# A two-layer hybrid trunk: a larger landing constant in the order planner, and another buffer for layer 2's SGU constants

## The chip, the cores and the metric

The kernel runs on one core of one Trainium2 chip. The metric is the device time of one execution in microseconds, the median of several runs. Four engines compute: TensorE (PE, whose weight loads the profile lists apart as PEld), VectorE (DVE), ScalarE (ACT) and GpSimd (POOL). SyncE (SP) issues all transfers of the program, and each engine works through its own queue in the order in which the program was written.

## The reference

Two layers act on 512 latent positions (x) and 256 context positions (ctx), with 1024 channels. The second layer still reads the context but does not produce it anew. Each layer computes, cut to what matters:

```python
h = x * (1 + scale) + shift                  # scale, shift, gate from silu(c) @ w_ada
parts = split(h @ w_in)                      # q,k,v, GLA, SGU and merge-gate columns
y_attn = attention(q, concat(k_ctx, k), concat(v_ctx, v)) * silu(a_g)
y_gla  = rms_norm(gla_forward + gla_backward) * silu(g_g)
vn     = layer_norm(s_v, sgu_ln_g, sgu_ln_b)
y_sgu  = s_u * (einsum('gts,bnsgc->bntgc', sgu_w, vn) + sgu_b) * silu(s_g)
m = sigmoid(m_a)*(y_attn@w_br_attn) + sigmoid(m_g)*(y_gla@w_br_gla) + sigmoid(m_s)*(y_sgu@w_br_sgu)
x_new = layer_norm(alpha * x + gate * (m @ w_out), post_g, post_b)
```

All of it is float32 in and out.

## The kernel before

**Matmuls.** Each float32 operand is split into a high part and a low rest in the matmul's faster float32 form, and each product is made of three matmuls (hi·hi, hi·lo, lo·hi; `mm3`). A weight slab is 256 rows by 256 columns (256 KB). `wgroup` loads it into one of three `raw` buffers, ACT writes `hi`, DVE writes `lo`, and after that the raw buffer takes the next slab; `hi` and `lo` have five buffers each.

**Order of the work.** Nothing is issued as it is written. The class `Sched` records every instruction with its reads, writes and a reckoned duration (`_cost`), and `Sched.order` simulates the five engines: at each step the engine that is free first takes the ready instruction with the smallest priority. 16 rounds are run (`issue`); after each the priorities move towards the latest start times of that round, and the round with the shortest reckoned end is issued. The order on every engine's queue is thereby fixed; on the chip an instruction at the head of a queue waits for its semaphores, and everything behind it on that engine waits too. A transfer is reckoned like this (L325 to L328; `cost` is bytes / 335 ns):

```python
            if e == "SP":
                dma = max(dma, st + 1300.0) + cost
                free[e] = max(st + 60.0, dma - self.AHEAD)
                end = dma + 700.0
```

`end` is when the readers of the loaded tile may start, and when a buffer whose last use is a store comes free. What else reads `end` is the backward pass that makes the latest start times.

**Places.** SBUF tiles live in places named by tags (`T(tag, ...)`), each with a fixed number of buffers (`BUFS`, L515: `hc` 2, `raw` 3, `S3` 8, most others 1). Tiles take the buffers of a tag strictly in the order in which the code first uses them; a tile whose tag is full waits until an earlier one has had its last use. What bears on the change:

- `T3` (one buffer), layer 2: `yat` (L909, the attention's output, until it is split into `yh` and `yl` for its projection), then `sgc` (L1226), then `mac0` (L1254, the first half of the merge's sum), then `pg` (L1375).
- `hc` (two buffers): the high and low half of the context's modulated rows (`new_h`, L707; layer 2's are `hch` and `hcl`, read by layer 2's projections for keys, values and GLA), and after them, in layer 2, `pgx` (L1313, the post-norm constants of layer 1).
- `T1`: `gv` (GLA's values) and then `ymix` (the SGU's result). `T5`: `kT`, then `sv` (the SGU's input read back from DRAM), then the merge's second half.
- `S3` (eight buffers): among much else, in this order, the kept gate rows read back from DRAM: 4 of `agd`, 4 of `ggd`, 4 of `sud`, 4 of `sgd` (all named `kept`), and then, for the first branch of the merge, rows of w_ada (`wada`) and `kept` from `md` (the gate rows of the merge's first branch).

**The SGU and the merge of a layer.** `sgc` holds four rows of constants, `lg`, `lb`, `bs` and `wsT`, each a transfer of 256 KB. For each of four 128-position tiles DVE makes statistics of `sv`, subtracts and scales, multiplies by `lg` and adds `lb` (both `sv<-sv,sgc`); PE multiplies by `wsT` (`pt<-sgc,sv`); DVE adds `bs` into `ymix`. Then `ymix` is multiplied by `kept` of `sud` and of `sgd`. The merge's first branch multiplies the projection of `yat` by the sigmoid of `kept` from `md` into `mac0`. Rows of w_ada are multiplied on DVE beside the merge (`ada_dot`: `prod` and `wada`).

The page's line numbers are those of helpers for most instructions (L421 records a call, L128 one of two engines' choice, L119 a group of matmuls), so the views are read by tile names.

Of the kernel before, what the change touches and what calls it, by code (L numbers as in the profile page):

```python
# [22 lines left out]
C_GQ, C_GK, C_GV, C_GG = 1280, 1536, 1792, 2336  # L23
C_SU, C_SV, C_SG = 2848, 3360, 3872
C_MA, C_MG, C_MS = 4384, 5408, 6432


class Sched:
# [109 lines left out]
    def order(self, prio):  # L138
# [31 lines left out]
        dma, cur, ticks, acted = 0.0, None, {}, 0.0  # L170
# [45 lines left out]
        while done < n:  # L216
# [108 lines left out]
            if e == "SP":  # L325
                dma = max(dma, st + 1300.0) + cost
                free[e] = max(st + 60.0, dma - self.AHEAD)
                end = dma + 700.0  # L328
            else:
                end = free[e] = st + cost  # L330
                if e == "ACT":
                    acted = end
                if e in held and e in self.port[i]:
                    held[e] = end
# [170 lines left out]
def kernel(ctx: ExitStack, tc: tile.TileContext, A, out, dbg=None):  # L505
# [11 lines left out]
    def T(tag, shape, dt=F32, name=None):  # L517
        return sc.tile(sb, shape, dt, tag, BUFS.get(tag, 1), name or tag, "SB")
# [192 lines left out]
    def layer(l, X, start=None):  # L711
        full = l == 0
# [510 lines left out]

        lab(f"{l}sgu")

        sgc = T("T3", [128, 4, 512], name="sgc")  # L1226
        lg, lb, bs, wsT = (sgc[:, i] for i in range(4))
        SP.dma_start(out=lg, in_=A["sgu_ln_g"][l].partition_broadcast(128))
        SP.dma_start(out=lb, in_=A["sgu_ln_b"][l].partition_broadcast(128))
# [227 lines left out]
    def start0():  # L1457
# [100 lines left out]
        return st_b  # L1558

    X1 = layer(0, X0, start0)  # L1560
    layer(1, X1)
    with tc.manual_schedule():
        a = 0
# [73 lines left out]
```

## Time and profile before

| | |
|---|---|
| median of 3 runs | 1430.35 us (1429.0 to 1435.49) |
| the profiled execution's own time | 1431.16 us |
| its span, first to last instruction | 1429.3 us |
| mean granted TensorE clock | 0.996 |
| instructions | 27382 |
| moved by transfers | 168.55 MB, mean 118 GB/s |

The layers follow one another: layer 1's start, attention and GLA until about 450 us, its merge and output until about 850, then layer 2's attention until about 1025, its GLA until about 1165, its SGU and merge until about 1380 and its output to the end. An engine's idle time in brackets, with an arrow and a name, is how long the engine stood still before that instruction and what ended it. Matmuls are pipelined, their ends are modelled; a PE that counts as busy may still run at the lower of its two clock levels, which a row of a window shows as PEclk.

### The profile page before, as it was taken

What the parts mean: (1) busy time and instruction counts of PE and PEld (TensorE: products, weight loads), DVE (VectorE), ACT (ScalarE), POOL (GpSimd) and SP (SyncE); (2) the same over time, 40 slices, a digit from 0 to 9 for tenths busy, and PEclk for the clock granted to TensorE, in tenths of its full rate; (3) what the DMA queues carried; (4) which work ended last, traced back from release to release, by engine and by line L of the source; (5) the groups of instructions that cost most, each with busy time, mean ns of one, the idle gap of its engine ahead of it and who ended that gap; (6) DMA issues with size and microseconds to landing.
All of it is one profiled execution on the core that took longest, in us unless ns stands there. A gap on an engine that the chain in (4) does not pass through costs nothing.

```text
span 1429.3 us, 27382 instructions
## 1 busy us (share of the span) xinstructions
PE 1387.9 (97%) x10724; PEld 1227.5 (86%) x10724; DVE 1032.5 (72%) x2206; ACT 671.3 (47%) x1293; POOL 164.5 (12%) x261
## 2 busy tenths in 40 slices
PE   8999999999999999999999999999999998999997
PEld 5798899987888888888889999998987877888887
DVE  8968877897977678732147684897799876645396
ACT  4566667844464323212232174666774554422331
POOL 0021100034330000000000020110014320000003
PEclk9999999999999999999999999999999999999999
DMA  9410012332356765521224232112243467535542
GB/s 321 160 45 9 23 31 65 124 94 64 93 177 207 250 200 169 158 67 45 65 77 148 66 119 71 30 31 60 82 148 90 117 193 252 168 97 177 182 144 94
DMA packets 123956, 168.55 MB, mean 118 GB/s; under 512 B 9497, under 2 KB 90801, under 8 KB 123825
## 3 DMA queue, kind: packets, MB, share of 16 engines
q1 hardware_dynamic: 123826, 166.79, 37.4%
q8 instruction: 84, 1.38, 0.4%
q14 instruction: 46, 0.38, 0.1%
HBM read 143.41 MB, written 23.34 MB: 117 GB/s over the span
## 4 chain that ended last, share of the span: by engine, by line
PE 73%; DVE 16%; DMA 5%; issue 2%; ACT 2%; POOL 1%; SPq 0%; POOLq 0%; DVEq 0%; ACTq 0%
PE p L421 60%; PE pt L421 8%; PE s L421 4%; DVE M L128 3%; DVE lo L128 2%; DMA wada<-in_w_adaT_dram 2%; DVE wada L421 1%; DVE sm L421 1%; DVE junk L421 1%; DMA raw<-in_w_in_dram 1%; PE s L119 1%; DVE PTs L421 1%; DMA sgc<-in_sgu_b_dram 1%; DVE cs L421 1%; POOL sf L421 0%
## 5 line engine op out<-in xcount | busy, mean ns | idle before, releaser
L128 DVE TENSOR_TENSOR lo<-raw,hi 128x512 fp32r<-128x512 f32 (+1 forms) x293 | 202.4, 700 | 173.7 <-ACT hi L421 166.2
L421 ACT ACTIVATE hi<-raw 128x512 fp32r<-128x512 f32 (+1 forms) x296 | 185.8, 634 | 233.2 <-PE p L421 149.8
L421 PE MATMUL p<-hlh,hi 128*128 128x512 f32 x704 | 280.9, 399 | 2.5 <-DVE mac L421 1.5
L421 PE MATMUL p<-hlh,lo 128*128 128x512 f32 x704 | 280.7, 399 | 1.5 <-DVE lo L128 1.3
L421 PE MATMUL p<-hll,hi 128*128 128x512 f32 x704 | 278.6, 396 | 0.0
L421 PEld LDWEIGHTS p<-hlh,lo 128*128 128x128 f32 x704 | 132.4, 188 | 31.6 <-DVE lo L128 2.1
L421 PEld LDWEIGHTS p<-hlh,hi 128*128 128x128 f32 x704 | 132.3, 188 | 29.8 <-ACT hi L421 2.2
L421 PEld LDWEIGHTS p<-hll,hi 128*128 128x128 f32 x704 | 132.3, 188 | 26.5
L421 PE MATMUL p<-hch,lo 128*128 128x256 f32 x368 | 104.5, 284 | 0.0
L421 PE MATMUL p<-hch,hi 128*128 128x256 f32 x368 | 104.2, 283 | 0.0
L421 PE MATMUL p<-hcl,hi 128*128 128x256 f32 x368 | 104.0, 283 | 0.0
L421 PE MATMUL p<-hi,hlh 128*128 128x256 f32 (+1 forms) x352 | 102.0, 290 | 0.0
L421 PE MATMUL p<-hi,hll 128*128 128x256 f32 (+1 forms) x352 | 100.8, 286 | 0.0
L421 PE MATMUL p<-lo,hlh 128*128 128x256 f32 (+1 forms) x352 | 99.8, 284 | 0.0
L421 POOL TENSOR_SCALAR sf<-sf 128x1 f32<-128x1 f32 x20 | 7.5, 374 | 642.3 <-DVE sf L421 641.9
L421 PE MATMUL p<-yh,hi 128*128 128x512 f32 (+1 forms) x192 | 70.0, 364 | 7.8 <-DVE mac L421 6.7
L421 ACT ACTIVATE P<-s,sm 128x768 f32<-128x768 f32 (+1 forms) x80 | 65.4, 821 | 23.5 <-DVE sm L421 23.2
L421 DVE TENSOR_REDUCE sm<-s 128x1 f32<-128x768 f32 (+1 forms) x72 | 65.0, 921 | 12.4 <-PE s L421 12.2
L421 DVE TENSOR_TENSOR PTs<-pt,PTs 128x512 fp32r<-128x512 f32 x104 | 69.2, 685 | 4.1 <-ACT PTs L421 3.1
L421 PEld LDWEIGHTS p<-hcl,hi 128*128 128x128 f32 x368 | 69.3, 188 | 2.1
L421 PEld LDWEIGHTS p<-hch,hi 128*128 128x128 f32 x368 | 69.5, 189 | 1.9
L421 DVE SCALAR_TENSOR_TENSOR wada<-wada,srow 128x512 f32<-128x512 f32 x96 | 65.1, 687 | 8.0 <-DMA wada<-in_w_adaT_dram 6.7
(299 smaller groups left out, 3352.1 us busy)
## 6 DMA issues: line engine op xcount, KB each, us to landing
raw<-in_w_in_dram SPq DMA_DIRECT2D x204, 256.0 KB, 3.0
wada<-in_w_adaT_dram SPq DMA_DIRECT2D x80, 256.0 KB, 4.9
raw<-in_w_out_dram SPq DMA_DIRECT2D x32, 256.0 KB, 2.9
raw<-in_w_in_dram SPq DMA_DIRECT2D x16, 272.0 KB, 3.1
wada<-in_w_adaT_dram SPq DMA_DIRECT2D x8, 512.0 KB, 4.9
raw<-in_w_br_attn_dram SPq DMA_DIRECT2D x16, 256.0 KB, 3.4
raw<-in_w_br_gla_dram SPq DMA_DIRECT2D x16, 256.0 KB, 3.0
raw<-in_w_br_sgu_dram SPq DMA_DIRECT2D x16, 256.0 KB, 3.3
```

Of the source, the lines that this page charges most:

```text
L119: return self.record(eng.n, lambda: [getattr(eng.e, m)(*a, **k) for m, a, k in calls], outs, ins, cost, None, dens)
L128: fns[p.n] = lambda real=real, k=k: real(**k)
L421: return s.record(n, lambda: real(*a, **k), outs, ins, _cost(n, meth, outs, ins, k), _table(n, k), _dens(n, ins, k), _port(n, meth, outs, ...
```

## The change

Two edits. A transfer's landing is reckoned at 2000 ns after its bytes have passed, where it was 700. And in layer 2 (`full` is true in layer 1 alone) `sgc` takes a buffer of `hc`, where it took `T3`; in layer 1 it stays in `T3`. What is computed, the number of instructions of each engine, and the transfers are the same; the planner runs anew, so the order of any queue may differ anywhere.

```diff
+LAND = 2000.0
@@ class Sched, order
             if e == "SP":
                 dma = max(dma, st + 1300.0) + cost
                 free[e] = max(st + 60.0, dma - self.AHEAD)
-                end = dma + 700.0
+                end = dma + LAND
@@ layer
-        sgc = T("T3", [128, 4, 512], name="sgc")
+        sgc = T("T3" if full else "hc", [128, 4, 512], name="sgc")
         lg, lb, bs, wsT = (sgc[:, i] for i in range(4))
```

## Rows read from the trace of the kernel before

**Rows 1.** The page, part 1: busy us, share of the span, instructions by engine.

```profile
PE 1387.9 (97%) x10724; PEld 1227.5 (86%) x10724; DVE 1032.5 (72%) x2206; ACT 671.3 (47%) x1293; POOL 164.5 (12%) x261
```

**Rows 2.** Waits of PE: who waited for whom: total us, times, longest.

```profile
PE p L421 <- DVE mac L421: 8.2, 4, 5.2
...
PE p L421 <- DVE rA L421: 0.2, 1, 0.2
```

**Rows 3.** Timeline, 1203 to 1213 us: start, us, engine, line, instruction [idle before].

```profile
1205.70 0.93 SPq L421 DMA_DIRECT2D kept<-md  x2
...
1209.23 1.28 ACT L421 ACT_TABLE_LOAD   x1 [2.02 <-DMA kept<-md]
...
1211.18 1.29 DVE L421 TENSOR_TENSOR mac<-p,kept 128x512 f32<-128x512 f32 x2 [0.69 <-ACT kept L421]
...
1211.93 0.80 PE L421 MATMUL p<-yh,hi 128*128 128x512 f32 x1 [5.21 <-DVE mac L421]
```

**Rows 4.** Windows around it: us, busy by engine, PEclk, DMA share, GB/s.

```profile
1205.00:1210.00 5.00, 1.71 (x8) 1.06 (x6) 5.00 (x10) 2.04 (x3) 0.00 (x0) 0.98 0.78 261
1210.00:1215.00 5.00, 3.07 (x7) 2.51 (x8) 3.74 (x10) 2.16 (x4) 0.00 (x0) 0.50 0.97 330
1215.00:1220.00 5.00, 5.00 (x20) 3.98 (x19) 1.39 (x3) 1.59 (x4) 0.00 (x0) 0.84 0.37 143
```

**Rows 5.** Single tiles in layer 2: ns min/median/max, first and last start us, forms.

```profile
L128 DVE TENSOR_TENSOR yl<-yat,yh x4: 682/684/686, 1172.4 to 1176.4; 128x512 fp32r<-128x512 f32 x4
...
L421 SPq DMA_DIRECT2D sgc<-in_sgu_ln_g_dram x1: 382/382/382, 1177.6 to 1177.6; - x1
...
L128 DVE TENSOR_TENSOR sv<-sv,sgc x8: 682/686/693, 1182.1 to 1189.7; 128x512 f32<-128x512 f32 x8
...
L421 DVE TENSOR_SCALAR sv<-sv,sf x4: 535/538/549, 1085.5 to 1106.8; 128x512 f32<-128x512 f32 x4
...
L421 DVE TENSOR_TENSOR ymix<-pt,sgc x4: 684/688/692, 1199.0 to 1203.1; 128x512 f32<-128x512 f32 x4
...
L421 PE MATMUL s<-gv,Af x24: 271/275/275, 1107.0 to 1164.0; 128*128 128x128 f32 x24
...
L421 PE MATMUL p<-hcl,hi x16: 277/282/286, 959.5 to 981.9; 128*128 128x256 f32 x16
```

**Rows 6.** Windows of attention, GLA and merge in layer 2, columns as in rows 4.

```profile
950.00:1000.00 50.00, 49.14 (x329) 43.94 (x328) 40.27 (x78) 32.75 (x65) 8.56 (x8) 1.00 0.17 47
...
1107.00:1164.00 57.00, 56.52 (x711) 46.03 (x710) 47.50 (x117) 27.14 (x52) 19.22 (x34) 1.00 0.40 110
...
1250.00:1300.00 50.00, 50.00 (x218) 40.54 (x217) 20.36 (x31) 14.63 (x24) 0.00 (x0) 1.00 0.35 95
```

**Rows 7.** The page, part 6: transfers, count, KB each, median us to landing.

```profile
raw<-in_w_in_dram SPq DMA_DIRECT2D x204, 256.0 KB, 3.0
wada<-in_w_adaT_dram SPq DMA_DIRECT2D x80, 256.0 KB, 4.9
```

**Rows 8.** Timelines of PE alone: five waits elsewhere, idle in brackets.

```profile
345.19 0.71 PE L119 MATMUL s<-M 64*32 64x64 f32 x48 [1.42 <-DVE M L128]
...
389.97 0.71 PE L119 MATMUL s<-M 64*32 64x64 f32 x48 [1.40 <-DVE M L128]
...
515.76 0.50 PE L421 MATMUL p<-yh,hi 128*128 128x512 f32 x1 [1.50 <-DVE mac L421]
...
534.02 0.47 PE L421 MATMUL p<-hlh,hi 128*128 128x512 f32 x1 [0.76 <-DVE mac L421]
...
608.15 0.50 PE L421 MATMUL p<-yh,hi 128*128 128x512 f32 x1 [0.99 <-DVE sig L421]
```

**Rows 9.** Chain that ended last, in order of time: start, us, what.

```profile
338.37 4.05 DMA raw<-in_w_in_dram
...
602.04 3.93 DMA pkl<-in_pkl_dram
```

**Rows 10.** The page, part 5: the split of slabs on ACT: busy us, mean ns, idle before.

```profile
L421 ACT ACTIVATE hi<-raw 128x512 fp32r<-128x512 f32 (+1 forms) x296 | 185.8, 634 | 233.2 <-PE p L421 149.8
```

## The prediction

> **What bounds the kernel now.** I read the page's busy shares first: PE is busy for 97% of the span and no other engine for more than 72% [rows 1]. The change adds and removes no work, so a gain can only come out of time in which PE stands still or runs slow. Second, the waits of PE. The list has 19 rows, from 8.2 us down to 0.2 (the first and the last are [rows 2]), 31.9 us added up: the most that any new order could win from visible waits, 2.2% of the time. The reader is to see how uneven it is: one wait of 5.2 us makes up a sixth. Third, the timeline around that wait and the windows over it; fourth, for the other waits, the chain of work, which shows what the engine that PE waits for had itself waited for.
>
> The longest wait stands in layer 2, where the SGU hands over to the merge. PE stops at about 1206.7 and goes on at 1211.93, 5.21 us later [rows 3]. It waits for DVE to empty a PSUM buffer into `mac`; that waits for ACT's sigmoid of `kept`; that waits for `kept<-md`, issued at 1205.70, after which ACT still loads a table of 1.28 us [rows 3]. The wait has a second price. After it the granted clock is 0.50 in 1210 to 1215 and 0.84 in 1215 to 1220 [rows 4], so PE, idle before, comes back at 1.2 GHz. In the 3.07 us for which it was busy in the first of these stretches it did half the work, which loses 1.5 us; in the second the lost share is 0.16 of 5 us, 0.8 us. So this one hole costs 5.2 + 2.3 = 7.5 us.
>
> **Why the transfer was late.** `kept<-md` sits in `S3` behind the eight `kept` of `sud` and `sgd`, whose buffers come free when `ymix` has been multiplied with them; `ymix` is written from 1199.0 to 1203.1 [rows 5]. Its place `T1` was free much earlier: the last matmul that reads `gv` starts at 1164.0. Its input was scaled long before, at 1106.8 at the latest. What was missing was `sgc`: its first transfer is issued at 1177.6, right behind the last `yl<-yat,yh` at 1176.4 plus its 0.68 us, the last use of `yat` in `T3` [rows 5]. Only then could DVE do the eight `sv<-sv,sgc` (1182.1 to 1189.7).
>
> **The second edit, sgc in hc.** Removed: the wait of `sgc` for `yat`, and of `mac0` for `sgc`. The two buffers of `hc` come free after the last matmul on `hcl`, at 981.9 [rows 5]; `sgc` takes one, `pgx` the other.
> - The four transfers (4 x 256 KB) move from 1177.6 to any time from 982 on. SP issues them ahead of or among weight slabs; at the 330 GB/s of the busiest stretch [rows 4] their 1.05 MB take 3.2 us. What hides it: the 950 to 1000 stretch has a DMA share of 0.17 [rows 6], and five `hi`/`lo` buffers stand between a late slab and PE. If that cover is gone, it costs at most those 3.2 us, once. Queued behind them on SP are `pgx` and slabs. I take 0. They also leave the crowded queue after 1177.
> - The eight multiplications and additions by `sgc`, 8 x 0.686 = 5.5 us of DVE [rows 5], move from after GLA into it. DVE is busy there for 47.50 of 57 us [rows 6], so 9.5 us are free: 0, and 5.5 us if they land ahead of what GLA waits for.
> - `ymix` may start when `gv` is free, at about 1165 instead of 1199; the `S3` buffers come free, and `kept<-md` starts, up to that much earlier. 5.2 us are needed, some 30 are offered. Bounds: nothing, if the planner leaves the SGU where it is, and the whole hole with its clock, 7.5 us. With six times what is needed I take the upper end: **-7.5 us**. Next late would be the last rows of GLA's output, which hold two `S3` buffers.
>
> **The first edit, LAND.** A lone slab of 256 KB is reckoned at 1.3 + 0.78 + 0.7 = 2.78 us from issue to landing (0.78 is 262144 bytes at 335 per ns); the new figure is 4.08. The trace has a median of 3.0 for slabs of w_in and 4.9 for rows of w_ada [rows 7]. So readers were placed at the head of in-order queues too early, where they hold up what is behind them. Six PE waits outside the hole go back to just that, 6.8 us together ([rows 8] are five of them; one more like that at 534 stands at 560, of 0.73): at 345 and 390 ACT stood before `hi<-raw` with GLA's exponential behind it; at 515, 534 and 560 DVE stood before a product with `wada`, with the merge's `mac` behind it; at 608 before the small constants of layer 2, with `sig` behind. The transfers took 4.05 us for the first and 3.93 for the last [rows 9]. A reader placed 1.3 us later has 1.3 us of other work ahead of it, so each PE wait can shrink by at most 1.3: 1.3 + 1.3 + 1.3 + 0.76 + 0.73 + 0.99 = 6.4 us at one end, and nothing at the other, if nothing else is ready. I take the three whose transfers are slabs or constants, where about 4.0 lies at the new figure: 1.3 + 1.3 + 1.0 = **-3.6 us**. For the three behind `wada` the median of 4.9 lies beyond it, and I book nothing.
>
> The same constant delays reckoned readers everywhere. A slab's round through its raw buffer is 3.0 to land, 0.63 for the split on ACT [rows 10], some 0.69 on DVE as in the like `yl<-yat,yh` [rows 5], and 0.4 allowed for the waits between: 4.7 us, or 1.6 us a slab over three buffers; 1.3 us more make it 2.0. PE uses a layer-2 slab in 12 matmuls: 218 touched the 50 us of 1250 to 1300 [rows 6], so about 2.8 us a slab. That hides it, with 2.4 us of the round to spare (3 x 2.8 less 6.0); if that is gone, each slab costs a third of what its round is over 8.4. I take 0. Buffers whose last use is a store are reckoned free 1.3 us later too; `keep` has three of them, with 24 matmuls and more between stores: 0. The start of the kernel, where transfers queue, may be ordered otherwise, and so may all the waits left over, 31.9 - 5.2 - 6.8 = 19.9 us: I take 0, with 8 us (two fifths of them) as what a luckier order could add to the gain, and 3 us for a loss.
>
> **A rule against it.** The trace shows slabs landing after 3.0 us in the median, near the old 2.78 and well below 4.08 [rows 7]. The Trainium skill, "DMA: Bandwidth & Descriptors", section on the anatomy of one DMA, gives a transfer as about 2.0 us fixed plus bytes over 436 GB/s, fitted on the GpSimd path. By that a slab is an estimated 2.6 us, the old figure is right for it and the new one 1.5 us too late; the landing term would be 0 and the sum -7.5. The measured tail at the stalls, 4.05 and 3.93, speaks against taking the lone figure there [rows 9].
>
> **Sum.** -7.5 - 3.6 = -11.1 us. The profiled execution took 1431.16 us (span 1429.3), 0.8 above the median of the runs: 1431.16 - 11.1 = 1420.1, less 0.8: **1419 us**.
>
> **Rivals.**
> - *Only the place works* (readers were early only where it cost nothing, or shift among equals). For: the median slab lands near the old figure [rows 7]. Against: the six waits [rows 8]. 1431.2 - 7.5 - 0.8 = 1423, on the border of what can be told.
> - *Only the landing works*: the hole stays because the planner still puts the SGU last, its transposes and matmuls having low rank beside projections. For: `sv` was complete at 1190.4 and `ymix` still came only at 1199.0 [rows 5]. 1431.2 - 3.6 - 0.8 = 1427.
> - *Nothing comes of it*: the planner keeps the round with the shortest end by its own figures, and the waits it removes reappear elsewhere, so that neither edit does what it says. 1430.
> - *Slower*: the 5.5 us of `sgc` work go into GLA, on the engine that GLA waits for. Its place is 1107 to 1164; it decides once DVE has fewer than 5.5 us free ahead of GLA's chain, where 9.5 are free in all. GLA then ends 5.5 us later, the SGU chain with it, and PE, out of projections, drops its clock once more (2.3): 1431.2 + 5.5 + 2.3 - 0.8 = 1438. For: in layer 1 PE twice waits for GLA's `M` on DVE [rows 8]. Against: PE is busy for 56.5 of these 57 us [rows 6], so its projections still cover.
>
> **How the numbers follow.** Both parts 0.45, only the place 0.20, only the landing 0.10, nothing 0.10, slower 0.15. About 0.5% (7 us) is what a measurement of this kernel can tell from no change. Faster by more: 0.45 plus half of the second, 0.55. Within: 0.10 + 0.10 + 0.10 = 0.30. Slower: 0.15. The range: low, 7.5 + 6.4 + 8 below 1431.2, less 0.8, gives 1408.5, so 1409; high, the nothing case plus 3 for a worse order, 1433. It leaves out the slower case and the ends. The likeliest case's own range is 1409 to 1423.
>
> **What would show it.** `sgc` transfers between 982 and 1107; `sv<-sv,sgc` before 1165; `ymix` before 1190; no PE wait on `mac` over 2 us and a clock of 1.00 throughout the merge of layer 2; the waits at 345, 390 and 608 gone or under 0.3; PE's waits summing to some 23 us. Wrong if a hole with a clock of 0.50 stands at the merge's start again, if the waits on GLA's `M` in layer 2 grow past 5 us, or if PE's waits stay above 30 us.

## The result and the profile after

The changed kernel takes 1418.27 us (median of 4 runs, 1416.74 to 1419.57) against 1432.71 for the kernel before in the same comparison: a ratio of 0.990, 95% interval 0.9871 to 0.993. The profiled execution took 1417.93 us with a span of 1416.1, 13.2 us less than before. 1419 had been forecast.

The page's busy shares answer to [rows 1]; the first rows of PE's waits answer to [rows 2]. The changed kernel is three lines longer, so its L424, L131 and L122 are L421, L128 and L119 of before.

```profile
PE 1385.3 (98%) x10724; PEld 1225.8 (87%) x10724; DVE 1039.8 (73%) x2229; ACT 679.1 (48%) x1298; POOL 150.6 (11%) x237
```

```profile
PE s L424 <- ACT hlh L424: 5.3, 5, 1.4
PE pt L424 <- DVE PTs L424: 2.9, 5, 0.9
PE s L122 <- DVE M L131: 2.4, 2, 1.5
```

The number of PE's instructions is the same. That of the other engines is not, against what stands ahead of the prediction: for some operations the planner also chooses the engine. POOL has 24 instructions fewer, 19 of them `M<-cs` of the GLA, and DVE has 23 more; ACT has 5 more, four of them table loads.

The 15 rows of PE's waits add up to 21.4 us where 19 rows made 31.9, so 10.5 us of visible waiting are gone; no row on `mac` is left. With the 2.3 us that the low clock was estimated to cost after the hole, that makes 12.8 of the 13.2 us.

The single tiles of layer 2, as in [rows 5], show the new order: constants loaded right after `hcl` is done, multiplied inside the GLA, the last of the SGU's result written 37 us earlier than before.

```profile
L424 SPq DMA_DIRECT2D sgc<-in_sgu_ln_g_dram x1: 341/341/341, 986.0 to 986.0; - x1
...
L131 DVE TENSOR_TENSOR sv<-sv,sgc x8: 679/683/693, 1088.5 to 1131.8; 128x512 f32<-128x512 f32 x8
...
L424 DVE TENSOR_TENSOR ymix<-pt,sgc x4: 680/680/681, 1160.7 to 1166.1; 128x512 f32<-128x512 f32 x4
```

In the timeline, `kept<-md` starts at 1171.96, and the merge's first `mac` comes at 1196.6, long after it. Two windows, one over the merge of layer 1 and one over the merge's start in layer 2, are the measure for all runs below. They lie at fixed times from the span's start, so a run that is some us ahead shows slightly later work in them (us, then busy time and instructions of PE, PEld, DVE, ACT and POOL, then granted clock, DMA share, GB/s). First the kernel before, then the changed one:

```profile
450.00:650.00 200.00, 195.60 (x1116) 170.00 (x1115) 130.05 (x319) 58.76 (x104) 0.24 (x1) 1.00 0.51 160
1190.00:1240.00 50.00, 44.79 (x203) 36.62 (x202) 31.15 (x62) 18.41 (x30) 0.00 (x0) 0.93 0.67 215
```

```profile
450.00:650.00 200.00, 200.00 (x1153) 175.13 (x1152) 134.75 (x324) 60.03 (x108) 0.00 (x0) 1.00 0.53 161
1190.00:1240.00 50.00, 50.00 (x218) 40.56 (x217) 31.52 (x62) 20.80 (x36) 0.00 (x0) 1.00 0.61 183
```

PE is busy for all of both. In the first it stood still for 4.4 us before, in the second for 5.2, with a mean clock of 0.93. Not all stretches won: in 890 to 1000 (attention of layer 2) PE was busy for 107.33 us before and is for 106.43 now, in 300 to 450 (GLA of layer 1) for 145.26 before and 144.33 now.

### The profile page after: what moved, and what is told of

Read it like the earlier page. It is cut to its first block, busy times and chain, and to the rows that moved or that the text cites. A ratio compares the mean times of both kernels' runs of the same rounds, so it can differ in the third digit from the quotient of the medians.

```text
span 1416.1 us, 27332 instructions
## 1 busy us (share of the span) xinstructions
PE 1385.3 (98%) x10724; PEld 1225.8 (87%) x10724; DVE 1039.8 (73%) x2229; ACT 679.1 (48%) x1298; POOL 150.6 (11%) x237
## 4 chain that ended last, share of the span: by engine, by line
PE 77%; DVE 13%; ACT 5%; issue 3%; POOL 1%; DMA 1%; SPq 0%; POOLq 0%; DVEq 0%; ACTq 0%
PE p L424 64%; PE pt L424 8%; PE s L424 4%; DVE M L131 2%; DVE lo L131 1%; ACT L424 1%; PE s L122 1%; ACT ez L424 1%; DVE sm L424 1%; DVE junk L424 1%; DVE PTs L424 1%; DVE wada L424 1%; DVE St L424 1%; DMA raw<-in_w_in_dram 1%; ACT hi L424 1%
## 5 line engine op out<-in xcount | busy, mean ns | idle before, releaser
L131 DVE TENSOR_TENSOR lo<-raw,hi 128x512 fp32r<-128x512 f32 (+1 forms) x294 | 203.2, 699 | 182.7 <-ACT hi L424 181.3
L424 ACT ACTIVATE hi<-raw 128x512 fp32r<-128x512 f32 (+1 forms) x296 | 185.6, 634 | 216.8 <-PE p L424 143.7
L424 PE MATMUL p<-hlh,hi 128*128 128x512 f32 x704 | 280.1, 398 | 0.3 <-ACT keep L131 0.3
L424 PE MATMUL p<-hll,hi 128*128 128x512 f32 x704 | 280.3, 398 | 0.0
L424 PE MATMUL p<-hlh,lo 128*128 128x512 f32 x704 | 279.8, 398 | 0.0
L424 PEld LDWEIGHTS p<-hlh,lo 128*128 128x128 f32 x704 | 132.4, 188 | 28.5
L424 PEld LDWEIGHTS p<-hll,hi 128*128 128x128 f32 x704 | 132.3, 188 | 26.7
L424 PEld LDWEIGHTS p<-hlh,hi 128*128 128x128 f32 x704 | 132.4, 188 | 26.5 <-ACT keep L131 0.5
L424 PE MATMUL p<-hch,lo 128*128 128x256 f32 x368 | 104.3, 283 | 0.0
L424 PE MATMUL p<-hch,hi 128*128 128x256 f32 x368 | 104.1, 283 | 0.0
L424 PE MATMUL p<-hcl,hi 128*128 128x256 f32 x368 | 103.9, 282 | 0.0
L424 PE MATMUL p<-hi,hlh 128*128 128x256 f32 (+1 forms) x352 | 101.7, 289 | 0.0
L424 PE MATMUL p<-hi,hll 128*128 128x256 f32 (+1 forms) x352 | 100.5, 286 | 0.0
L424 PE MATMUL p<-lo,hlh 128*128 128x256 f32 (+1 forms) x352 | 100.2, 285 | 0.0
L424 POOL TENSOR_SCALAR sf<-sf 128x1 f32<-128x1 f32 x20 | 7.0, 352 | 665.2 <-DVE sf L424 664.6
L424 ACT ACTIVATE P<-s,sm 128x768 f32<-128x768 f32 (+1 forms) x80 | 65.4, 821 | 23.4 <-DVE sm L424 23.1
L424 DVE TENSOR_TENSOR PTs<-pt,PTs 128x512 fp32r<-128x512 f32 x104 | 69.4, 685 | 4.3 <-ACT PTs L424 3.2
L424 PEld LDWEIGHTS p<-hch,hi 128*128 128x128 f32 x368 | 69.5, 189 | 2.2
L424 PEld LDWEIGHTS p<-hcl,hi 128*128 128x128 f32 x368 | 69.3, 188 | 2.2
L424 DVE TENSOR_REDUCE sm<-s 128x1 f32<-128x768 f32 (+1 forms) x72 | 64.8, 920 | 7.5 <-PE s L424 7.3
L424 PEld LDWEIGHTS p<-hch,lo 128*128 128x128 f32 x368 | 69.2, 188 | 0.2
L424 PE MATMUL p<-yh,hi 128*128 128x512 f32 (+1 forms) x192 | 68.6, 357 | 0.0
```

What stands on the lines that cost most here:

```text
L131: fns[p.n] = lambda real=real, k=k: real(**k)
L424: return s.record(n, lambda: real(*a, **k), outs, ins, _cost(n, meth, outs, ins, k), _table(n, k), _dens(n, ins, k), _port(n, meth, outs, ...
```

## The experiments

In each run the ratio is to the kernel before on the same chip, with a 95% interval. There are four such comparisons, in which the kernel before took 1432.71 us (changed kernel), 1430.89 (e1 to e4), 1432.41 (e5 to e8) and 1431.79 (e9 to e12). A difference in us across two of them can therefore be off by some 2 us; the ratios are the safer measure. "Merge 1" is PE's busy time in the 200 us from 450; "merge 2" that in the 50 us from 1190, with the mean clock.

| run | constants | landing ns | median us | ratio [interval] | merge 1 | merge 2 |
|---|---|---|---|---|---|---|
| changed kernel | hc | 2000 | 1418.27 | 0.990 [0.9871, 0.993] | 200.00 | 50.00, 1.00 |
| e1 | T3 | 2000 | 1426.75 | 0.9973 [0.9963, 0.9984] | 199.70 | 45.72, 0.93 |
| e2 | hc | 700 | 1441.25 | 1.0064 [1.0049, 1.0079] | 196.04 | 38.33, 0.86 |
| e3 | T3 | 720 | 1435.08 | 1.0031 [1.0021, 1.0041] | 195.69 | 44.57, 0.93 |
| e4 | hc | 1950 | 1424.78 | 0.9954 [0.9942, 0.9966] | 198.88 | 44.87, 0.93 |
| e5 | hc, SGU put first | 700 | 1434.45 | 1.0016 [1.0006, 1.0026] | 197.48 | 46.38, 1.00 |
| e6 | hc, SGU put first | 1950 | 1418.2 | 0.9897 [0.9883, 0.9912] | 198.79 | 50.00, 1.00 |
| e7 | T3 | 2000 for w_ada, else 700 | 1424.94 | 0.9946 [0.9934, 0.9958] | 199.68 | 44.35, 0.93 |
| e8 | T3 | 3300 | 1438.75 | 1.0049 [1.0033, 1.0064] | 193.49 | 45.03, 0.93 |
| e9 | T3 | 700 for w_ada, else 2000 | 1424.97 | 0.9950 [0.9938, 0.9962] | 199.32 | 45.86, 0.97 |
| e10 | hc, SGU put first | as e7 | 1425.05 | 0.9946 [0.9934, 0.9959] | 199.74 | 49.53, 1.00 |
| e11 | hc | as e7 | 1433.59 | 1.0011 [1.0001, 1.0021] | 199.90 | 39.89, 0.83 |
| e12 | hc, loaded late | 2000 | 1422.24 | 0.9934 [0.9923, 0.9946] | 199.91 | 45.60, 0.97 |

### One part alone: e1 and e2

e1, from the changed kernel:

```diff
-        sgc = T("T3" if full else "hc", [128, 4, 512], name="sgc")
+        sgc = T("T3", [128, 4, 512], name="sgc")
```

> Landing reckoned at 2000 ns, but layer 2's SGU constants stay in T3 behind the attention's output. Theory (two parts that add up): the hole at the merge's start in layer 2 is still there with a clock near 0.5 after it, the waits behind late transfers in layer 1 are gone; 3.6 to 6.4 us faster than before, about 1427, some 8 us slower than the changed kernel. Rival (the landing does it all): the hole goes too, about 1418. Rival (the place does it all): no change, 1431.

1426.75 us. As the theory had it: merge 1 has lost its waits and merge 2 has the hole, in PE's timeline:

```profile
1205.14 0.79 PE L424 MATMUL p<-yh,hi 128*128 128x512 f32 x1 [4.28 <-DVE mac L424]
```

e2, from the changed kernel:

```diff
-LAND = 2000.0
+LAND = 700.0
```

> Layer 2's SGU constants in hc, landing reckoned at 700 ns as before. Theory (two parts): the constants are loaded at about 985 us, the result of the SGU is written before 1190, no PE wait over 2 us at the merge's start; 7.5 us faster than before, about 1424; five or six waits of 0.7 to 1.5 us behind late transfers in layer 1 stay. Rival (the place does it all): about 1418. Rival (the landing does it all): 1431.

1441.25 us: neither theory; slower than before by 0.64%. The place did what it says, the constants are loaded from 981 us on and multiplied from 1088 to 1117. But the GLA's end moved behind everything else. The last two groups of matmuls on `gv`:

```profile
L424 PE MATMUL s<-gv,Af x16: 271/275/275, 1152.2 to 1198.1; 128*128 128x128 f32 x16
```

In the kernel before the last started at 1164.0. PE had used up its projections, stood 3.58 us for the norm of the GLA's last group, and then 7.87 for `mac`. The clock fell twice, to 0.75 in 1200 to 1205 and to 0.50 in 1220 to 1225:

```profile
1202.18 0.86 PE L424 MATMUL pt<-ident,o 128*128 128x128 f32 x4 [3.58 <-DVE o L424]
...
1222.02 0.80 PE L424 MATMUL p<-yh,hi 128*128 128x512 f32 x1 [7.87 <-DVE mac L424]
```

So, given constants that come early, the planner put the GLA's last group behind the projections. Why the planner's reckoning preferred this order was not tested.

### What a new plan alone does: e3 and e4

e3 and e4 change the figure by a hair:

```diff
-LAND = 2000.0
+LAND = 720.0      # e3, with sgc in T3
+LAND = 1950.0     # e4, with sgc in hc
```

> The kernel before with the landing reckoned at 720 ns instead of 700: a change that is nothing to the chip but makes the planner run anew. Theory: within 3 us of before, the hole at the merge's start of layer 2 still there. Rival (luck of the plan: any new plan scatters by as much as the change gained): more than 6 us from before in either direction.

> The changed kernel with the landing reckoned at 1950 ns instead of 2000. Theory: within 3 us of the changed kernel, about 1418, with no hole in layer 2 and no waits behind w_ada rows in layer 1. Rival (luck of the plan): more than 6 us from it.

1435.08 us, 0.31% above before for 20 ns more; and 1424.78, 6.5 us above the changed kernel for 50 ns less. The first lies between the theory and the rival, and the hole is still there (5.4 us); the second lies on the rival's side. In e4 the four SGU tiles start as early as in the changed kernel, and three are written by 1165.3, but the plan leaves the last of them to 1193, and the hole is back:

```profile
L424 DVE TENSOR_TENSOR ymix<-pt,sgc x4: 674/684/692, 1160.5 to 1193.1; 128x512 f32<-128x512 f32 x4
```

```profile
1203.27 0.80 PE L424 MATMUL p<-yh,hi 128*128 128x512 f32 x1 [4.65 <-DVE mac L424]
```

An early load makes an early SGU possible; it does not make the planner use it.

### The order put in by hand: e5 and e6

The planner is told, and only the planner, that the projections behind the last two thirds of layer 2's early merge gates follow the SGU's result (`first` is the number of instructions recorded before a gate):

```diff
+            if not full and j >= 1:
+                held += [k for k in range(first, len(sc.ops)) if sc.ops[k][0] == "PE"]
...
-            tt(DVE, ymix[:, :, qtile(t)], ps, ...)
+            k = tt(DVE, ymix[:, :, qtile(t)], ps, ...)
+            for j in held:
+                sc.ops[j][2].add(k)
```

> Landing 700, constants in hc, and the planner alone is told that the last two thirds of layer 2's early merge-gate projections come after the SGU's result. Theory (hc only makes an early SGU possible, and the rank of these projections decides whether the planner uses it): the GLA ends near 1165 instead of 1198, no PE wait over 2 us and no clock near 0.5 at the merge's start; the layer-1 merge keeps its 5 to 7 us of waits; about 1424, 17 us faster than the place alone. Rival (the place is bad in itself, its transfers or its DVE work slow the GLA): stays within 4 us of 1441.

> The same order put on the kernel with landing 1950 and hc, which had a PE wait of 4.7 us at the merge's start. Theory: that wait goes with its clock, some 6 us; 1418 to 1420. Rival (the changed kernel's last 6 us came from elsewhere in its plan): stays near 1425.

e6 gives 1418.2 us, 6.6 less than e4: merge 2 is full at a clock of 1.00. So the hole is what e4 had lost against the changed kernel, and there the order of the SGU before these projections is enough to close it. e5 gives 1434.45, 6.8 less than e2 but not the 17 expected. Its hole at the merge is smaller (2.4 us at most), but now the held projections are missing while the GLA ends, at 1174:

```profile
1178.17 1.12 PE L424 MATMUL pt<-ident,o 128*128 128x128 f32 x4 [3.58 <-DVE o L424]
```

### Which transfers: e7, e8 and e9

```diff
-                end = dma + LAND
+                end = dma + (LAND if any("wada" in x for x in ops[i][3]) else 700.0)   # e7, T3
+                end = dma + (700.0 if any("wada" in x for x in ops[i][3]) else LAND)   # e9, T3
```

e8 sets LAND to 3300 with sgc in T3.

> Constants in T3; the landing reckoned at 2000 ns for the 88 transfers into w_ada rows alone and at 700 for all others. Theory (in layer 1's merge it is the products with w_ada rows that stand at the head of DVE's queue): PE's lost time between 450 and 650 us falls from about 7 to under 2.5, the waits at the SGU and merge of layer 2 stay; 1426 to 1429. Rival (the weight slabs matter): layer 1's merge keeps 6 us or more of lost time, 1430 or more.

> Constants in T3; the landing reckoned at 3300 ns. Theory (2000 already lies at the ninth tenth of what transfers need, so nothing more is to be won, and readers that come late cost elsewhere): layer 1's merge loses no more than 1 us, but the total is no better than with 2000, 1427 to 1433. Rival (the later the better): under 1423.

> Constants in T3; landing 2000 for every transfer but those into w_ada rows, which keep 700 (the complement of the run with 2000 for w_ada rows alone, 1424.9). Theory (w_ada rows carry the whole gain of the landing figure): PE loses 5 us or more between 450 and 650 us, and the attention of layer 2 loses some 2.5 us more than before, as with 2000 for all; 1431 to 1435. Rival (each kind carries its share): 1427 to 1429.

e7 took 1424.94 us, better than the 1426 to 1429 of its theory: a later landing for the 88 loads of w_ada rows alone empties merge 1 (199.68 of 200). But e9, the complement, took 1424.97, below both of its expected ranges, and empties it too (199.32), against the theory that w_ada rows carry the whole gain. It keeps one thing expected, in a smaller size: PE is busy for 106.39 us in 890 to 1000, as in the changed kernel, where e7 has 107.28 and before 107.33. So either half of the figure does, both together (e1, 0.9973) come out above either half, which is not explained, and the later slabs go with some 0.9 us more of waiting in the attention of layer 2.

The two halves do not work in the same way. The waits of DVE before products with w_ada rows, 450 to 650 (total us, times, longest), in the kernel before, e7, e9 and e2:

```profile
DVE prod L421 <- DMA wada<-in_w_adaT_dram: 30.1, 13, 6.8
DVE prod L424 <- DMA wada<-in_w_adaT_dram: 19.1, 8, 4.3
DVE prod L424 <- DMA wada<-in_w_adaT_dram: 23.4, 13, 5.4
DVE prod L424 <- DMA wada<-in_w_adaT_dram: 25.1, 14, 5.4
```

e9 leaves DVE standing there nearly as long as e2, yet PE loses 0.7 us of merge 1 in e9 and 4.0 in e2. Slabs reckoned later thus do not free these products. What in e9's plan keeps PE busy all the same is not shown.

e8's theory has its ninth tenth from the trace: reckoned by the planner's rule from the issue times of the kernel before, the transfers whose landing is on record land 0.95 us after their bytes in the median, and 2.0 at the ninth tenth. But 3300 is too much: 1438.75 us, worse than with 2000 and outside both ranges. Merge 1 loses 6.5 us, where the theory allowed 1: ACT waits 8.59 us there for `kept<-md`, and PE behind it:

```profile
531.94 0.80 PE L424 MATMUL p<-yh,hi 128*128 128x512 f32 x1 [5.57 <-DVE mac L424]
```

### Both gains without the later slabs: e10 and e11

e11 is e7's line with sgc in hc; e10 adds the order of e5.

> Constants in hc, 2000 for w_ada rows alone, and the SGU put before the last two thirds of the early merge-gate projections. Theory: the layer-1 merge loses under 2 us, no PE wait over 2 us at the merge of layer 2, and the attention of layer 2 does not pay; 1416 to 1419. Rival (with hc the GLA of layer 2 ends late unless weight slabs are reckoned late too, as in the two runs with hc and 700): 1424 to 1430, with a PE wait on the GLA's output.

> Constants in hc and 2000 for w_ada rows alone, nothing else forced. Theory: whether the hole at the merge of layer 2 closes is the planner's choice, so 1417 with the SGU's result written before 1180, or 1425 and more with it after 1190; the layer-1 merge loses under 2 us in both. Rival (hc with 700 for the slabs is bad in itself): the last group of the GLA comes after 1170 and the time is 1430 or more.

1425.05 and 1433.59 us. The rival holds in both: e11's last group of the GLA starts its last matmul at 1190.5, and e10 stops PE at the GLA's end. With this wait the clock falls to 0.59 in 1170 to 1175 (PE busy for 2.82 us) and 0.72 in 1175 to 1180 (4.86 us). Priced as in the prediction, that loses some 2.5 us, so the wait costs an estimated 6.1 of the 6.8 us between e10 and the changed kernel.

```profile
1172.13 1.12 PE L424 MATMUL pt<-ident,o 128*128 128x128 f32 x4 [3.58 <-DVE o L424]
```

All four runs with hc and 700 for the slabs (e2, e5, e10, e11) have this wait of 3.58 us; none of the four with hc and 1950 or 2000 (the changed kernel, e4, e6, e12) has it. So in these plans the two edits of the change lean on each other.

### Early load or a free T3: e12

```diff
+        last = len(sc.ops)                      # behind the split of yat
...
+        if not full:
+            for k in late:                      # the four loads of sgc
+                sc.ops[k][2].update(j for j in range(last - 8, last))
```

> The changed kernel, but the planner is told that layer 2's four loads of constants come after the last split of the attention's output, as T3 forced it before. mac0 still has T3 to itself. Theory (the early load is what closes the hole): the SGU's result is written after 1190 again, the PE wait of 4 to 5 us with a clock near 0.5 is back, 1425 to 1428. Rival (freeing T3 for the merge's sum is what closes it): no such wait, 1417 to 1420.

The constants are loaded from 1155.6 on, after the split, `ymix` is written from 1189.0 to 1191.9, and the hole is there although nothing stands between `yat` and `mac0` in `T3`:

```profile
1201.62 0.79 PE L424 MATMUL p<-yh,hi 128*128 128x512 f32 x1 [4.40 <-DVE mac L424]
```

So the freed place alone does not close the hole. The time is 1422.24 us, 4.0 above the changed kernel and below the 1425 expected.

That the late load forces the hole is not shown, though. In e12 DVE is through with the constants at 1167.6, and PE takes up their matmuls only 20 us later:

```profile
L131 DVE TENSOR_TENSOR sv<-sv,sgc x8: 684/686/694, 1161.1 to 1166.9; 128x512 f32<-128x512 f32 x8
L424 PE MATMUL pt<-sgc,sv x32: 272/275/275, 1187.9 to 1191.6; 128*128 128x128 f32 x32
```

The same gap is 16 us in e1 and 7 in the kernel before. So in e12, as in e4, it is the plan that leaves the SGU lying. The rival that the order alone would close the hole, with the constants loaded late or left in `T3`, was not run.

## Why the prediction was right, and where it was not

**The total held, and all signs of the profile but one.** 1419 was forecast and 1418.27 measured; PE's waits were to sum to some 23 us and sum to 21.4; constants at 986.0, `ymix` at 1166 at the latest, no wait on `mac`, a clock of 1.00 at the merge of layer 2. One sign failed: the wait at 390 was to be gone or under 0.3, and is 1.49.

**The hole's mechanism held, from the SGU's result on.** Where the last write of `ymix` starts by 1180 (the changed kernel, e6, e10), PE waits at most 0.3 us for `mac` at the merge's start in layer 2; in e5, at 1187, the longest wait is 2.4; in the ten others, the kernel before among them, from 1192 on, it is 4.1 to 7.9. The price of 7.5 us is met by e1 against the changed kernel, 8.5 (10.4 by the ratios), and by e4 against e6, 6.6 (8.2 by the ratios). The step before it, that the late `sgc` was what held the result back, is shown only as far as no run with a late load has an early result; e1 and e12 had their constants in time and left them lying.

**"With six times what is needed I take the upper end" was too sure.** The step took the time offered for the time used. The planner decides, and of the four runs with an early load and no order put in (the changed kernel, e2, e4, e11) only the changed kernel used it; e2 and e11 even end the GLA later, at 1198 and 1190. As a term of its own, -7.5 for the place, it failed: the place alone costs 0.64%. The rival "only the place works", at 1423, is refuted; the loss did not come in the way of the slower rival either. Its 5.5 us of DVE work do sit in the GLA, but what e2 lost stands at the GLA's end, where its last group was put behind the projections.

**The landing's term had the right size for a wrong reason.** Booked were 3.6 us from two waits of the GLA in layer 1 and one at 608; e1 measured 0.27%, 3.9 us. But of the two GLA waits one is still there, and 300 to 450 as a whole did not gain. ACT before that wait, in the kernel before and the changed one, and then PE in the changed one:

```profile
387.47 0.63 ACT L421 ACTIVATE hi<-raw 128x512 fp32r<-128x512 f32 x1 [2.18 <-DMA raw<-in_w_in_dram]
...
387.50 0.85 ACT L424 ACTIVATE M<-M 128x768 f32<-128x768 f32 x1 [0.97 <-DVE M L131]
...
389.67 0.71 PE L122 MATMUL s<-M 64*32 64x64 f32 x48 [1.49 <-DVE M L131]
```

The slab no longer holds up the GLA's exponential (`M<-M`) there, as the edit meant; but ACT now waits for DVE's `M`, and PE stands as long as before.

What went are the waits behind w_ada rows, for which nothing was booked, and the one at 608: 4.4 us of merge 1. The step that failed is "for the three behind `wada` the median of 4.9 lies beyond it": DVE still stands before the products with w_ada rows (17.2 us in merge 1 where it stood 30.1), but it now comes to `mac` before PE is done, where PE had to wait for it. A wait need not vanish; it has to fall under the slack behind it. In part the rows themselves came sooner: their median to landing is 4.3 us, where it was 4.9; how much that gave is not shown. The waits of DVE, 450 to 650 (total us, times, longest), in the changed kernel, and those before `mac` there and in the kernel before:

```profile
DVE prod L424 <- DMA wada<-in_w_adaT_dram: 17.2, 9, 3.9
DVE mac L424 <- PE p L424: 4.5, 5, 1.2
...
DVE mac L421 <- PE p L421: 0.4, 1, 0.4
```

**The rule weighed against it.** By the Trainium skill, "DMA: Bandwidth & Descriptors", section on the anatomy of one DMA, a transfer on the GpSimd path takes about 2.0 us plus its bytes over 436 GB/s, an estimated 2.6 us for a slab. By that the old figure was right for a lone slab, and the landing's term came to 0. Slabs, which SP issues here, took 3.0 us in the median before and after, near enough to the estimate; yet e1 gained 0.27% [0.16%, 0.37%]. The gain came in merge 1, where DMA is busy for half of the time and rows of w_ada land later than that [rows 7].

**Luck.** Steps of 20 and 50 ns moved the time by 4.2 and 6.5 us. Parts of 4 and 8 us cannot be told from such scatter by their time alone; merge 1 and merge 2, read stage by stage, can. That the changed kernel drew a plan that uses the early load was not foreseeable from the trace before.

## What to carry to other kernels

Where a planner writes the order, moving a tile only offers it a choice: read in the new trace whether it was taken, and, if the choice matters, write the order down, as e6 did for 6.6 us. Judge an edit of a planner's figure by the stage it is meant for, and run a neighbour of the figure before believing the total. Of the landing figures tried for all transfers, 2000 ns emptied the crowded stretch of PE's waits, 1950 left 1.1 to 1.2 us, and 720 and 3300 left 4.3 and 6.5.

## What the runs showed that was not expected

The norm of the GLA's last group, from the square on ACT over DVE and POOL back to DVE, cost PE 3.58 us in four different plans, the same to the last digit given, each time with no projections placed in between. And not every hole had a second price: in the runs whose longest wait on `mac` was 4.1 us or more the mean clock of merge 2 was 0.83 to 0.97 (in e2 and e11 the wait of 3.58 us lies in it too); in e5, with 2.4 us at most, it stayed at 1.00, while its 3.58 us at 1178 left a clock of 0.78 in 1175 to 1180 and 0.88 in 1180 to 1185.
